# TensorE in the program's order in both mixers of a hybrid encoder layer, with other work dealt out between half steps

## The chip, the cores and the metric

The kernel runs on one NeuronCore of a Trainium2 chip. The metric is the device time of one launch in microseconds; lower is better.

## The reference, cut to what matters

One encoder layer over 1024 tokens of width 1024, in float32. The change touches the two attention mixers and the work that runs beside them.

```python
u = rms_norm(h); qa, ka, va, qb, kb, vb = split(u @ w_in)     # 1024 x 2304
# mixer A: 8 query heads, 2 key heads of 64, normed, rotary, over all keys
sc = einsum('bkgqd,bksd->bkgqs', qblk, k) * scale
oa = rms_norm(einsum('bkgqs,bksd->bkgqd', softmax(sc), v))
# mixer B: 8 heads, three dilated windows (128,1), (512,4), (2048,16), merged by their denominators
ob = rms_norm(einsum('pbhs,pbhsd->bhsd', softmax(lses), outs))
h = h + concat(oa, ob) @ w_out
h = h + hierarchical_moe(rms_norm(h))                          # 32 experts
y = rms_norm(h)
```

## The kernel before, in words

Every float32 matmul operand is split into a high and a low part (`split`: ScalarE copies the high part at L131, VectorE subtracts at L140), and a product is three (or two) matmuls. The program is written through Tile: the author traces instructions in program order, and the scheduler sets each engine's order from a simulated timeline, so that an instruction may pass earlier ones that are not ready in that simulation. `tc.manual_schedule(engines={PE})` around a region makes TensorE keep the program's order there; the routing and the experts behind the mixers (L1068 and L1250) already stand in such regions. The other engines' orders, and the DMA queues', are the scheduler's in either case.

The work before and in the mixers is written as Python generators, and a `yield` is a place where another generator may be let in.

- `job(n, jp)` (L254) projects one chunk of 256 columns of `w_in` for two tiles of tokens: 8 pieces of 6 matmuls of 256 columns each (L261 to L263), a `yield` after each, then the evacuation, the rotary on VectorE (L234, L237, L238) and the splits, and a last `yield`. Chunks 0 and 1 are run before the mixers, 4 jobs each; `rest_of_projection` runs the other 7, so 7 x 4 x 9 = 252 yields.
- Mixer A, `prepare_a` (from L489): turns a head's queries (L303, two pieces), finds each row's maximum over the keys (L499 matmul and L500 VectorE maximum, 8 pieces of two), then `shifts` makes the negative maximum (L333 to L335) and turns it in (two pieces). 12 yields a head.
- Mixer A, `steps_a`: a head has 16 steps (two blocks of 512 queries by 8 key tiles). `front` computes scores (L518, L519), ScalarE takes the exponential `p` and its high part `ph`, VectorE or GpSimd the low part `pl` (L445), GpSimd the running sum (L529). `back` multiplies the values (L536, L537). At kt = 7 it copies the block's output to `o` on ScalarE and turns it back right away, 4 times L543 and L544, then divides.
- Mixer B is alike: `prepare_b` (turning keys and queries, maxima L642 and L644; for head 0 the loads of `load_b`, L620 and L621, and then IDLE = 3 empty yields), `finish_b` (L662, L670, L673, then the shifts), and 8 steps a head: 4 strided ones (`front_c`, `back_c`), 4 windowed ones (`front_w`, `back_w`). The scores are masked on VectorE (L691), then `p` and `ph` on ScalarE, `pl` on GpSimd (L696). After the last window the sums are added (L762) and `divided` turns them (L740).
- `first_half` multiplies A's outputs by the first half of `w_out` (L827): 78 yields, 64 of them 3 matmuls of 512 columns.

`attend(n, stages, steps, ahead, pace)` (L448) weaves them: the stages of the first heads are run at once, then each step runs its `front`, the `back` of the step two before (ahead = 2), and `pace` pieces of the coming heads' preparation, and then yields once. `pace` is 1 in A and 3 in B. Around it stand three loops: A's turns with the projections (L555 on), RATE = 2.3 pieces a turn; A's remaining turns with one call into B's `attend` each (L770 on); B's turns with RATE_O = 1.0 piece of `first_half` each (L858 on), and then the rest of `first_half`.

[...]

Of the kernel before, what the change touches and what calls it, by code (L numbers as in the profile page):

```python
# [32 lines left out]
RATE = 2.3  # L33
# [7 lines left out]
RATE_O = 1.0  # L41
# [84 lines left out]
def tile_encoder(ctx, tc, I, out):  # L126
# [28 lines left out]
    turn = itertools.cycle(("i0", "i1"))  # L155
# [138 lines left out]
    def run(g):  # L294
        for _ in g:
            pass
# [70 lines left out]
    for j in range(NT):  # L367
        x, ss, _ = rows_x[j]
# [48 lines left out]
    def rest_of_projection():  # L417
        for n in range(2, 9):
            if n not in w_raw:
                load_chunk(n)  # L420
            split_chunk(n)
            if n + 1 < 9:
                load_chunk(n + 1)
            for jp in range(4):
                yield from job(n, jp)
# [3 lines left out]
    part = {"pl": SH_P, "s": 1.0}  # L429
# [18 lines left out]
    def attend(n, stages, steps, ahead, pace):  # L448


        state, at = {}, {}

        def stage(k, h):
            state[h] = yield from stages[k](h, state.get(h))

        def advance(g, times):
            for _ in range(times):
                if next(g, g) is g:
                    return False
            return True  # L460

        d = len(stages)
        for h in range(d):
            for k in range(d - h):
                yield from stage(k, h)
        waiting = []
        for h in range(n):
            coming = [stage(d - 1 - a, h + 1 + a) for a in range(d) if h + 1 + a < n]
            for front, back in steps(h, state.pop(h)):
                front()  # L470
                waiting.append(back)
                if len(waiting) > ahead:
                    waiting.pop(0)()
                for _ in range(pace):
                    if coming:
                        g = coming.pop(0)
                        if advance(g, 1):
                            coming.append(g)
                yield
            for g in coming:  # L480
                yield from g
        for back in waiting:
            back()
# [69 lines left out]


    turns = attend(8, [prepare_a], steps_a, 2, 1)  # L555
    side = rest_of_projection()
    due = 0.0
    while side is not None:
        next(turns, None)
        due += RATE  # L560
        while due >= 1:
            due -= 1
            if next(side, side) is side:
                side = None
                break
    part.update(pl=SH_P2, s=SH_S2)
    inx.close()
    obp = ctx.enter_context(tc.tile_pool(name="obp", bufs=1, side="right"))
# [116 lines left out]
    def steps_b(h, state):  # L685
# [61 lines left out]
        def back_w(j0):  # L747
# [20 lines left out]
            [(lambda j=j: front_w(j), lambda j=j: back_w(j)) for j in range(0, NT, 2)]  # L768

    side = attend(8, [prepare_b, finish_b], steps_b, 2, 3)  # L770
    for _ in turns:
        next(side, None)
    att.close()


# [55 lines left out]
    def first_half():  # L831
        for k in range(2):
            load_out(k)
        A.dma_start(g_o[0], _all(I["out_norm_a_g"], 512))
        A.dma_start(g_o[1], _all(I["out_norm_b_g"], 512))
        yield
        for k in range(4):
            split_out(k)
            if k < 3:
                load_out(2 + k)  # L840
            yield
        o = turned(q_a[:, 0], 0, "x")
        for j in range(NT):
            x = [wk_a.tile([P, 512], F32, name="x2") for _ in range(2)]
            for b in range(2):
                G.dma_start(x[b], _tokens(I["x"], j)[:, 512 * b:512 * b + 512])
            now = o
            if j + 1 < NT:
                o = turned(q_a[:, j + 1], 0, "x")
            yield  # L850
            for b, h in enumerate((q_a, h_b)):
                ps = bank("d", [P, 512])
                yield from half_product(0, now, ps, b)
                V.tensor_tensor(h[:, j], ps, x[b], op=OP.add)
        split_out(4)
        yield

    more, due = first_half(), 0.0  # L858
    for _ in side:
        due += RATE_O  # L860
        while due >= 1:
            due -= 1
            next(more, None)
    run(more)
    names.update(a="b", b="x", c="d", d="i1", s="i0")
    first_mixed = turned(o_b[0][:, 0], 1, "a")
    wka.close()
# [499 lines left out]
```

## Time and profile before

| what | us |
|---|---|
| median of 3 runs (1391.66 to 1401.73) | 1392.15 |
| the profiled execution | 1393.38 |
| its span, first to last instruction | 1391.7 |
| TensorE busy | 1303.2 |
| VectorE busy | 1152.4 |
| ScalarE busy | 926.2 |
| GpSimd busy | 568.6 |

A matmul's record runs from its start to its modelled end, and the next one starts before that end, so the time that a matmul takes from TensorE is the distance between starts. PE is TensorE's matmuls, PEld its weight loads, DVE VectorE, ACT ScalarE, POOL GpSimd, SP SyncE, whose queue issues most DMAs. L131 and L140 are helpers that many operations share, so their tiles tell them apart.

### The profile page before, as it was taken

The page shows a single profiled execution, that of the slowest core. Times are in us where ns is not written, and L with a number is a line of the kernel's source. Part 1 is how long each engine was busy: PE and PEld are TensorE (multiplying, and loading weights), DVE is VectorE, ACT ScalarE, POOL GpSimd, SP SyncE. Part 2 cuts the span into 40 slices and gives each one's busy share as a digit, 9 for nine tenths or more (in the row PEclk, how much of TensorE's full clock was granted, in tenths as well). Part 3 has the DMA queues.
Part 4 walks back from the last instruction along what each step waited for, and adds up shares of the span by engine and source line. Part 5 has one row for each costly group of instructions (what it writes and reads, how often), then busy time and mean ns, then how long its engine had stood idle before and what let it go on. Part 6 is the DMA issues. An engine that isn't in the chain of part 4 may idle for free. (4 is left out here: it accounts for less than half of the span.)

```text
span 1391.7 us, 21904 instructions
## 1 busy us (share of the span) xinstructions
PE 1303.2 (94%) x7333; PEld 1110.6 (80%) x7333; DVE 1152.4 (83%) x2001; ACT 926.2 (67%) x1366; POOL 568.6 (41%) x556
## 2 busy tenths in 40 slices
PE   5999899999998999999897999999999999999983
PEld 5999779888976889889686788878888888888862
DVE  5788997899868777667587799989999999999976
ACT  5334556655566656556443688878888888888873
POOL 5673566745566645446354611122111111111215
PEclk9999999999998999899998999999999999999997
DMA  7113321231242564445767999999999999999925
GB/s 258 62 39 85 84 68 54 61 75 36 58 138 60 145 186 117 112 128 164 278 210 240 308 371 367 353 341 372 360 351 351 345 360 355 349 353 342 376 74 226
DMA packets 213044, 299.63 MB, mean 215 GB/s; under 512 B 94307, under 2 KB 115939, under 8 KB 212928
## 3 DMA queue, kind: packets, MB, share of 16 engines
q1 hardware_dynamic: 200528, 272.91, 58.1%
q0 software_dynamic: 11968, 24.55, 6.7%
q8 instruction: 58, 0.95, 0.3%
q10 hardware_dynamic: 432, 0.75, 0.3%
q14 instruction: 58, 0.48, 0.1%
HBM read 267.85 MB, written 44.58 MB: 224 GB/s over the span
## 5 line engine op out<-in xcount | busy, mean ns | idle before, releaser
L140 DVE TENSOR_TENSOR wl<-unit,wh 128x1024 fp32r<-128x1024 f32 x140 | 168.4, 1223 | 21.1 <-ACT wh L131 20.1
L1163 POOL DMA_INDIRECT o_b<-xn_d,rows x32 | 51.4, 1606 | 303.1 <-PE ps_a L1180 300.8
L131 ACT ACTIVATE wh<-unit 128x1024 fp32r<-128x1024 f32 x140 | 147.3, 1062 | 36.3 <-PE ps_b L1196 12.5
L529 POOL TENSOR_TENSOR psum<-psum,p 128x512 f32<-128x512 f32 x93 | 138.0, 1484 | 66.7 <-ACT p L131 56.6
L263 PE MATMUL ps_i<-wih,ul 128*128 128x256 f32 x576 | 163.1, 283 | 1.2 <-DVE ul L140 1.2
L261 PE MATMUL ps_i<-wih,uh 128*128 128x256 f32 x576 | 162.7, 283 | 0.8 <-ACT uh L131 0.8
L262 PE MATMUL ps_i<-wil,uh 128*128 128x256 f32 x576 | 162.2, 282 | 0.0
L131 ACT ACTIVATE ph<-p 128x512 fp32r<-128x512 f32 x192 | 119.0, 630 | 12.7 <-DVE pl L445 5.7
L445 DVE TENSOR_TENSOR pl<-p,ph 128x512 fp32r<-128x512 f32 x93 | 96.1, 1035 | 24.7 <-ACT ph L131 24.6
L131 ACT ACTIVATE p<-ps_b 128x512 f32<-128x512 f32 x128 | 74.6, 595 | 62.2 <-PE ps_b L519 39.7
L261 PEld LDWEIGHTS ps_i<-wih,uh 128*128 128x128 f32 x576 | 109.6, 190 | 7.0 <-ACT uh L131 1.5
L262 PEld LDWEIGHTS ps_i<-wil,uh 128*128 128x128 f32 x576 | 109.4, 190 | 5.5
L263 PEld LDWEIGHTS ps_i<-wih,ul 128*128 128x128 f32 x576 | 109.5, 190 | 5.1 <-DVE ul L140 1.7
L696 POOL TENSOR_TENSOR pl<-p,ph 128x512 fp32r<-128x512 f32 x64 | 83.4, 1309 | 73.2 <-ACT ph L131 51.9
L1233 POOL DMA_INDIRECT y_d<-y,rows x31 | 50.3, 1622 | 137.5 <-ACT y L131 134.2
L140 DVE TENSOR_TENSOR wl<-rawc,wh 128x1024 fp32r<-128x1024 f32 x70 | 84.4, 1223 | 10.4 <-ACT wh L131 9.9
L500 DVE TENSOR_REDUCE m<-ps_x 128x1 f32<-128x512 f32 x128 | 84.9, 678 | 7.9 <-PE ps_x L499 7.6
L1196 PE MATMUL ps_b<-wh,x_hi 128*128 128x512 f32 x256 | 87.0, 421 | 0.0
L131 ACT ACTIVATE wh<-rawc 128x1024 fp32r<-128x1024 f32 x70 | 74.3, 1067 | 18.2 <-PE ps_b L1196 7.2
L1220 PE MATMUL ps_d<-wh,h_hi 128*128 128x512 f32 x256 | 81.0, 397 | 1.7 <-ACT h_hi L131 1.7
L1220 PE MATMUL ps_d<-wh,h_lo 128*128 128x512 f32 x256 | 81.1, 398 | 1.5 <-DVE h_lo L140 1.5
L1196 PE MATMUL ps_c<-wh,x_hi 128*128 128x512 f32 x256 | 80.9, 397 | 0.0
(326 smaller groups left out, 3888.9 us busy)
## 6 DMA issues: line engine op xcount, KB each, us to landing
unit<-in_w_up SPq DMA_DIRECT2D x49, 512.0 KB
unit<-in_w_gate SPq DMA_DIRECT2D x47, 512.0 KB
unit<-in_w_down SPq DMA_DIRECT2D x44, 512.0 KB
rawc<-in_w_gate SPq DMA_DIRECT2D x25, 512.0 KB
rawc<-in_w_down SPq DMA_DIRECT2D x23, 512.0 KB
rawc<-in_w_up SPq DMA_DIRECT2D x22, 512.0 KB
h_b<-in_w_down SPq DMA_DIRECT2D x19, 512.0 KB
raw<-in_w_in SPq DMA_DIRECT2D x36, 256.0 KB
```

What stands on the lines that cost most here:

```text
L131: A.activation(o, i, f, **kw)
L140: (eng or V).tensor_tensor(lo, src, hi, op=OP.subtract)
L261: T.matmul(ps[:, jj], u_hi[j][:, k], wh, start=(k == 0 and jj == 0), stop=False, skip_group_check=True)
L262: T.matmul(ps[:, jj], u_hi[j][:, k], wl, start=False, stop=False, skip_group_check=True)
L263: T.matmul(ps[:, jj], u_lo[j][:, k], wh, start=False, stop=(k == 7), skip_group_check=True)
L445: engine("pl").tensor_tensor(pl, p, ph, op=OP.subtract)
L500: V.tensor_reduce(m2[:, j, b:b + 1], ps, axis=AX.X, op=OP.max)
L529: engine("s").tensor_tensor(st["s"], st["s"], p, op=OP.add)
L696: G.tensor_tensor(pl, p, ph, op=OP.subtract)
L1163: gathers.append(G.indirect_dma_start(out=x_g, out_offset=None, in_=xn_d[:, :], in_offset=bass.IndirectOffsetOnAxis(ap=rows, axis=0), boun ...
L1196: T.matmul(st["gu"[n % 2]], lhs[:, k % 4], rhs[:, 512 * a:512 * a + 512], start=(k == 0 and i == 0), stop=(k == 7 and i == 2))
L1220: T.matmul(py[b], lhs[:, k], w[n][:, 512 * b:512 * b + 512], start=(k == 0 and i == 0), stop=(k == 3 and i == 2))
```

## The change

`attend` yields after each part of a step: with pace 1 the parts are front, piece, back; with pace 3 front, piece, back, piece, piece. The pieces thus stand between the halves, and what runs beside is let in after every part. The rates are divided by the number of parts, 3 in A's loop and 5 in B's, while the loop between the two calls B's `attend` once per part of A. IDLE stays 3. Around the three loops TensorE keeps the program's order.

```diff
--- before.py
+++ after.py
@@ -467,16 +467,20 @@
         for h in range(n):
             coming = [stage(d - 1 - a, h + 1 + a) for a in range(d) if h + 1 + a < n]
             for front, back in steps(h, state.pop(h)):
-                front()
                 waiting.append(back)
-                if len(waiting) > ahead:
-                    waiting.pop(0)()
-                for _ in range(pace):
+
+                def piece():
                     if coming:
                         g = coming.pop(0)
                         if advance(g, 1):
                             coming.append(g)
-                yield
+
+                turn = [front, lambda: waiting.pop(0)() if len(waiting) > ahead else None]
+                for i in range(pace):
+                    turn.insert(2 * i + 1, piece)
+                for part in turn:
+                    part()
+                    yield
             for g in coming:
                 yield from g
         for back in waiting:
@@ -555,14 +559,15 @@
     turns = attend(8, [prepare_a], steps_a, 2, 1)
     side = rest_of_projection()
     due = 0.0
-    while side is not None:
-        next(turns, None)
-        due += RATE
-        while due >= 1:
-            due -= 1
-            if next(side, side) is side:
-                side = None
-                break
+    with tc.manual_schedule(engines={mybir.EngineType.PE}):
+        while side is not None:
+            next(turns, None)
+            due += RATE / 3
+            while due >= 1:
+                due -= 1
+                if next(side, side) is side:
+                    side = None
+                    break
     part.update(pl=SH_P2, s=SH_S2)
     inx.close()
     obp = ctx.enter_context(tc.tile_pool(name="obp", bufs=1, side="right"))
@@ -768,8 +773,9 @@
             [(lambda j=j: front_w(j), lambda j=j: back_w(j)) for j in range(0, NT, 2)]
 
     side = attend(8, [prepare_b, finish_b], steps_b, 2, 3)
-    for _ in turns:
-        next(side, None)
+    with tc.manual_schedule(engines={mybir.EngineType.PE}):
+        for _ in turns:
+            next(side, None)
     att.close()
 
 
@@ -856,12 +862,13 @@
         yield
 
     more, due = first_half(), 0.0
-    for _ in side:
-        due += RATE_O
-        while due >= 1:
-            due -= 1
-            next(more, None)
-    run(more)
+    with tc.manual_schedule(engines={mybir.EngineType.PE}):
+        for _ in side:
+            due += RATE_O / 5
+            while due >= 1:
+                due -= 1
+                next(more, None)
+        run(more)
     names.update(a="b", b="x", c="d", d="i1", s="i0")
     first_mixed = turned(o_b[0][:, 0], 1, "a")
     wka.close()
```

## Rows read from the trace of the kernel before

**Rows 1.** The page, parts 1 and 2: busy time, and the clock of TensorE in 40 equal slices.

```profile
PE 1303.2 (94%) x7333; PEld 1110.6 (80%) x7333; DVE 1152.4 (83%) x2001; ACT 926.2 (67%) x1366; POOL 568.6 (41%) x556
...
PEclk9999999999998999899998999999999999999997
```

**Rows 2.** Stretch, length; busy us of PE, PEld, DVE, ACT, POOL; clock; DMA; GB/s.

```profile
95.60:165.70 70.10, 64.81 (x453) 58.83 (x453) 65.79 (x130) 31.55 (x57) 32.22 (x30) 0.98 0.37 83
165.70:393.40 227.70, 220.92 (x1501) 197.10 (x1500) 193.95 (x305) 140.15 (x249) 139.54 (x96) 1.00 0.24 58
393.40:451.80 58.40, 52.08 (x269) 39.88 (x268) 47.98 (x90) 40.15 (x73) 41.52 (x32) 0.91 0.39 109
451.80:660.80 209.00, 200.97 (x1255) 183.64 (x1255) 148.99 (x434) 127.29 (x219) 104.86 (x101) 0.93 0.53 141
660.80:680.90 20.10, 15.03 (x72) 11.70 (x70) 11.84 (x29) 8.56 (x14) 8.44 (x17) 0.83 0.75 244
```

**Rows 3.** Waits of PE, 130 to 681 us: total us, times, longest.

```profile
PE ps_x L499 <- DVE m L500: 5.1, 8, 1.8
PE ps_d L537 <- DVE pl L445: 4.4, 7, 1.2
...
PE ps_x L543 <- DVE m L500: 2.9, 1, 2.9
PE ps_b L705 <- DVE p L691: 2.9, 2, 1.6
...
PE ps_b L518 <- ACT p L131: 1.6, 2, 1.1
...
PE ps_b L731 <- DVE p L691: 0.3, 1, 0.3
```

**Rows 4.** Timeline from 396.8 us: start, us, engine, line, what.

```profile
396.86 0.40 PE L537 MATMUL ps_d<-pl,v_st 128*64 128x512 f32 x1
...
397.09 0.28 PE L261 MATMUL ps_i<-wih,uh 128*128 128x256 f32 x1
...
397.20 0.28 PE L262 MATMUL ps_i<-wil,uh 128*128 128x256 f32 x1
...
397.36 0.59 ACT L131 ACTIVATE o<-ps_d 128x512 f32<-128x512 f32 x1
...
398.72 0.33 PE L543 MATMUL ps_x<-eye,o 128*128 128x64 f32 x2
```

**Rows 5.** L263 by stretch (two are one piece), and the row maxima of head 0.

```profile
0.00:86.00 86.00, 44.98 (x154) 30.32 (x155) 0.96 0.42 142
86.00:104.00 18.00, 11.39 (x41) 7.58 (x41) 1.00 0.06 16
...
L500 DVE TENSOR_REDUCE m<-ps_x x18: 674/678/692, 91.2 to 125.0; 128x1 f32<-128x512 f32 x18
```

**Rows 6.** DMA issues, L518 and the DMA share when mixer B begins.

```profile
398.01 0.33 SPq L620 DMA_DIRECT2D keep<-bk_d  x1
...
393.40:422.90 29.50, 6.54 (x16) 3.03 (x16) 0.94 0.71 197
...
399.00:403.00 4.00, 4.00 (x29) 3.49 (x29) 2.79 (x6) 3.41 (x7) 3.44 (x3) 1.00 0.80 254
403.00:408.00 5.00, 4.89 (x21) 3.23 (x20) 5.00 (x9) 3.72 (x8) 3.59 (x3) 1.00 1.01 318
408.00:411.00 3.00, 2.68 (x11) 1.68 (x11) 3.00 (x5) 1.80 (x3) 1.68 (x4) 1.00 0.04 11
```

**Rows 7.** Groups by line and form between scores and weights in mixer B, 451 to 661 us.

```profile
L696 POOL TENSOR_TENSOR pl<-p,ph 128x512 fp32r<-128x512 f32 x62 | 80.8, 1309 | 71.9 <-ACT ph L131 50.5 <-issue 6.0 <-PE ps_i L720 3.6
L691 DVE TENSOR_TENSOR p<-ps_b,masks 128x512 f32<-128x512 f32 x63 | 43.2, 686 | 13.7 <-PE ps_b L706 7.4 <-POOL pl L696 3.7 <-PE ps_b L732 2.6
L131 ACT ACTIVATE ph<-p 128x512 fp32r<-128x512 f32 x67 | 41.6, 628 | 2.7 <-PE ps_i L720 1.6
...
L762 DVE TENSOR_TENSOR ob<-ob,ps_i 65x320 f32<-65x320 f32 x7 | 3.3, 475 | 0.2 <-PE ps_i L760 0.2
```

## The prediction, made before the changed kernel was built or run

> **What bounds the kernel now.** I read the page first, then the busy time by stretch, then the list of waits, and last the timeline at the places where the new order differs. The page [rows 1] says that TensorE is busy 94% of the span and that its granted clock stays near 9 tenths or full except in a few slices. The change touches only the mixers, so I cut them into five stretches [rows 2]: the start of mixer A (95.6 to 165.7 us), its steady part with projections beside it (165.7 to 393.4), the stretch in which A ends and mixer B is prepared (393.4 to 451.8), mixer B (451.8 to 660.8), and the end of the output product's first half (660.8 to 680.9). In the steady part TensorE is busy 220.92 of 227.70 us at full clock, VectorE 193.95. So TensorE is the bound there and waits only 3%. At the start VectorE is the fuller one (65.79 of 70.10). In B TensorE is busy 200.97 of 209.00 us, but at a mean clock of 0.93.
>
> What could be won is small. All waits that are put down to an instruction between 130 and 681 us sum to 30.5 us over 18 rows, the first and the last of which are shown, and five of them make 16.9 [rows 3]. [...]
>
> **The change part by part.** The work is the same, instruction for instruction; what moves is TensorE's order. Now the scheduler mixes: after the last value product of a block (L537 at 396.86) other matmuls go before the turning matmuls L543 at 398.72 that need its copy `o` [rows 4]. The change makes TensorE follow the program inside three regions, and the program has places where the next matmul needs what another engine makes from the one just before.
>
> *Turning the output of mixer A (`back`, kt = 7).* L543 stands right behind L537, with no yield between. In the shown case `o` ends 1.09 us after L537 starts (396.86 to 397.95) [rows 4]; L537 fills 0.23 of it (the spacing from it to L261), so TensorE stands 0.86 us, and about 0.05 for the signal. That is the floor. ScalarE is busy 61% of the steady part [rows 2], and a copy that finds `p` and `ph` ahead of it waits up to 1.2 us more. 16 blocks at 0.9 give 14 us, at 2.1 give 34; I take 1.1, near the floor since the shown case is an ordinary one: 18 us. Of it 2.9 us is paid already (L543) [rows 3], so **+15**.
>
> *The start of A.* In the order of before TensorE runs ahead with projections while VectorE prepares head 0. Two L263 make one piece (a `yield` of `job`), so 77 pieces are done by 86.0 us and 20.5 more from 86 to 104 [rows 5], where the program before the loop holds 2 chunks of 32 = 64. So 13 pieces were pulled ahead, and 34 are spent before 104. In the new order the preparation of head 0 has 12 yields, and each brings RATE/3 = 0.77 piece: 9 pieces. The 25 others are 150 matmuls of 0.115 us (the spacing of L261 and L262) [rows 4], 17 us without cover. Against that: the stretch is VectorE's. Its 16 row maxima cost 16 x 0.678 = 10.8 us [rows 5], and with fewer projections ahead fewer rotaries stand in its queue, so the first steps come earlier and the pieces serve as cover later. Both ends stand, 0 and 17; I take **+6**, nearer to 0 because VectorE, busy 65.79 of 70.10 us, is the fuller engine there.
>
> *The preparation of mixer B.* The loads of head 0 are issued from 398.0, right behind the last projection, and the DMA engines are full until 408 [rows 6]. They are hidden by IDLE = 3 empty yields. Before, a yield is one step of A, 1.84 us apart there (16 L518 in 29.5 us), so some 5.5 us, and what waits can be passed. After the change a yield is a third of a step, so the three cover 1.9 us, and the turning of the keys then stands at TensorE's head, with A's steps queued behind it. The keys are a quarter of the 2 MB, so they land some 2 us after the transfers begin at 399, the queries later. Between 0 and 408 - 398 - 3 = 7 us; I take **+4**.
>
> *The end of each head of B (`divided`).* The second group of transposes needs VectorE's add L762 of the last window, right behind L760: about 0.28 - 0.12 (a matmul of 256 columns and its spacing, as L261) + 0.48 (L762) + 0.1, less 0.24 for the first group's transposes, is 0.5 us [rows 4, 7]. Eight heads: **+4**, 0 to 10 with none of it or another VectorE operation ahead.
>
> *B's steps without pieces.* The 15 pieces of preparation fall, at 3 a step, into a head's first 5 steps. In the last 3 the way from scores to `pl` is 0.3 (matmul) + 0.69 (mask) + 0.63 (`p`, as long as `ph`) + 0.63 (`ph`) + 1.31 (`pl`) = 3.6 us and four signals [rows 7], and it is covered by two steps of some 1.9 us each, which the new order cannot lengthen. 24 steps at 0 to 0.7; I take 0.15: **+4**.
>
> *The row maxima's last piece*, after which the transposes of `shifts` and `finish_b` wait for four short VectorE operations, stands 16 times in the same order as before; those that were passed by other work now wait. 0 to 10, I take **+3**.
>
> *What goes away.* Fronts, pieces and backs now stand a third of a step apart with projections between them, so the waits for the maxima (L499, 5.1 us), for `pl` (L537, 4.4), for the masks' sums (L705, 2.9) and for `p` (L518, 1.6) should shrink [rows 3]; and TensorE standing elsewhere gives VectorE time. From 0 to -15; I take **-12**. The clock I leave at 0: even feeding would give back up to 23 us, new waits would cost up to 15.
>
> *The rates.* RATE/3 and RATE_O/5 keep the pieces per step. When the projection ends about 22 steps of A are left where it was 30 (252 pieces, less 9, at 2.3 a step), and three yields a step bring 67 calls into B, 26 of them its preparation and 41 for 8 steps; before, 30 calls, 4 steps. So 4 pieces more are left to the end, where one more half product stands: its matmuls are the same work, and its add (0.7 us) has the next tile's transposes beside it: 0, at most +2. DMA issues (the loads of `load_b`, `load_v`, of `x2`) stay in SP's and GpSimd's own orders, which the regions do not pin; they pass no other transfer by the change, and beyond the load above they are covered by a whole head.
>
> Sum: 15 + 6 + 4 + 4 + 4 + 3 - 12 = +24 us. The profiled execution took 1393.4 us around its span of 1391.7, 1.2 above the median of the runs shown (1392.15). So 1393.4 + 24 = 1417.4, which I give as 1417.
>
> The list of waits shows TensorE standing for L537 and L499 with work behind them that was ready [rows 3]. [...]
>
> **The rivals.** *Faster, 0.17.* Even feeding holds the clock in B. For it: half-speed stretches there are 14% of 209 us [rows 2], in stretches with little beside the steps, and the change deals the output product out at five places a step where it was one. Against it: the same light matmuls remain. With the clock's 23 us back, the waits 12 less, and only the turning (15) paid beside the start at 0, the sum is -20: 1373. It decides at a granted clock of 0.97 or more in B.
>
> *No change, 0.27.* In A VectorE is busy 85 to 94% [rows 2]: what TensorE loses at the turning and at the start it would have lost later waiting for maxima and `pl`. Then 15 + 6 fall away: 1393 + 3 = 1396. Against it: in the steady part TensorE waits only 7 us of 228, too little to hold 15.
>
> *Slower than forecast, 0.13.* The short waits in B pull the clock down. For it: B already falls to half speed while TensorE is busy 96% of the time [rows 2]. With 0.85 instead of 0.93 the 209 us become 229, and with 0.5 us at the 24 late steps +8 more: 1417 + 20 + 8 = 1445. [...]
>
> **How the numbers follow.** Forecast 0.43, faster 0.17, no change 0.27, slower still 0.13. A measurement of this kernel tells about 1% (14 us) from no change. Faster by over 1% is nearly all of the first rival and a little of the forecast's lower end: 0.17. Within 1%: most of the second and the forecast's lower part: 0.28. Slower: 0.55. The likeliest case alone runs from 1400 (turning at its floor, B's terms at 0) to 1440 (turning at 1.6 us, start at 12, load at 7). The range reaches from 1380, which leaves out most of the faster case, to 1458, the upper end of the slower one with its waits doubled.
>
> **What would show it.** Right: an L543 wait for `o` near 1 us in 16 places; about 9 pieces between the first maxima and the first front, and TensorE idle there; a wait of L303 for the key load at B's start; a shorter list for L499 and L537. Wrong: a granted clock of 0.97 in B, or a steady part of A no longer per step than now while L543 waits, which would mean that VectorE set its pace.

## The result, and the profile after

The changed kernel takes 1498.74 us (median of four runs, 1492.74 to 1504.82) where the kernel before, on the same chip, takes 1393.30: a ratio of 1.0744, 95% interval 1.067 to 1.0818. It is slower, as forecast, but by 105 us and not by 24. The profile is of a run of 1504.82 us, so it shows some 6 us more than the median.

In the changed kernel the lines below the diff stand 4 to 7 lower: L499, L518, L537 and L543 are now L503, L522, L541 and L547, and in mixer B L642, L662, L740 are L647, L667, L745. The page, parts 1 and 2, beside [rows 1]:

```profile
PE 1352.3 (90%) x7333; PEld 1146.5 (76%) x7333; DVE 1139.3 (76%) x1999; ACT 932.9 (62%) x1366; POOL 557.0 (37%) x558
...
PEclk9989898998999586999999979999999999999997
```

TensorE runs the same 7333 matmuls and is busy 49 us longer with them. Nothing was added, so they ran slower: in the first half, where the mixers are, the digits of the clock now show a 5, a 6 and five 8s, where they showed two 8s.

To see where, I cut both kernels at the same events, from 78 us, up to where the two run alike: the first scores of A, the last projection, the last value product of A, the last scores of B, and the last matmul of the output product's first half (L827, now L833). Columns as in [rows 2]. First the kernel before:

```profile
78.00:95.70 17.70, 17.70 (x149) 17.44 (x148) 15.50 (x40) 4.21 (x6) 13.37 (x19) 1.00 0.15 44
95.70:397.70 302.00, 289.93 (x1979) 259.63 (x1979) 260.60 (x434) 174.15 (x310) 173.52 (x127) 0.99 0.26 63
397.70:465.30 67.60, 61.28 (x314) 48.48 (x313) 56.22 (x111) 47.45 (x86) 50.98 (x38) 0.90 0.41 117
465.30:660.70 195.40, 187.37 (x1182) 171.16 (x1181) 139.79 (x413) 117.44 (x201) 93.45 (x92) 0.93 0.54 143
660.70:668.40 7.70, 7.70 (x44) 6.47 (x44) 3.58 (x5) 4.95 (x8) 3.08 (x3) 1.00 0.69 236
sum 590.40, PE 563.98 PEld 503.17 DVE 475.69 ACT 348.19 POOL 334.40; mean PE 112.80 PEld 100.63 DVE 95.14 ACT 69.64 POOL 66.88
```

And the changed one:

```profile
78.00:102.70 24.70, 14.20 (x81) 12.02 (x81) 17.84 (x38) 4.47 (x8) 5.67 (x8) 0.79 0.13 36
102.70:472.50 369.80, 337.61 (x2122) 297.27 (x2121) 267.49 (x459) 190.49 (x328) 185.64 (x146) 0.92 0.22 51
472.50:561.40 88.90, 71.40 (x346) 57.88 (x344) 49.81 (x136) 48.11 (x89) 41.30 (x35) 0.75 0.40 113
561.40:759.10 197.70, 170.29 (x1049) 157.26 (x1048) 120.05 (x360) 108.07 (x183) 85.61 (x85) 0.89 0.49 127
759.10:785.60 26.50, 21.27 (x98) 15.58 (x96) 10.97 (x27) 6.45 (x12) 10.22 (x21) 0.94 0.74 258
sum 707.60, PE 614.77 PEld 540.01 DVE 466.16 ACT 357.57 POOL 328.44; mean PE 122.95 PEld 108.00 DVE 93.23 ACT 71.52 POOL 65.69
```

The five stretches grew by 7.0, 67.8, 21.3, 2.3 and 18.8 us, 117.2 in all (the rest of the kernel is 5.7 shorter). B and what follows it belong together: B holds 133 matmuls fewer, 54 more are left behind it. The sum rows split the growth in two. TensorE is busy 614.77 us where it was 563.98, **51 us more** for almost the same matmuls (3696 and 3668): that is the clock. It stands still for 92.8 us (707.60 - 614.77) where it was 26.4, **66 us more**: those are waits. The clock column says the first part again. In both traces the clock stands at 1.00 or at 0.50: in the changed kernel it is 1.00 from 196 to 201 us, 0.50 from 201.5 to 204.5 and 1.00 from 205 to 210, in the kernel before 0.50 from 577 to 585 and 1.00 from 586 to 600. So 2 x (1 - clock) x length is the time at half speed: 59 us in the stretch of the projections, where it was 6, and 160 over all five, where it was 47; half of the difference, an estimate of 57 us, is lost.

The waits of PE from 78 to 800 us, total, times, longest; before they summed to 30.5 us [rows 3], now to 93.9. Of the accumulators in the mixers `ps_x` takes maxima and turnings, `ps_b` scores, `ps_d` the values of A, `ps_i` projections and later the values of B.

```profile
PE ps_x L547 <- ACT o L131: 23.8, 16, 4.5
PE ps_x L303 <- DVE keep L685: 12.3, 5, 5.1
PE ps_x L303 <- ACT q_st L131: 9.1, 1, 9.1
PE ps_x L503 <- DVE m L504: 6.8, 9, 2.1
PE ps_x L303 <- DVE q1b L685: 6.8, 3, 3.7
PE ps_x L303 <- DVE ql_st L335: 5.8, 4, 3.5
...
PE ps_x L667 <- DVE mx L663: 4.8, 2, 3.2
PE ps_i L745 <- DVE ob L767: 3.8, 8, 0.9
PE ps_x L647 <- DVE mc L649: 3.5, 1, 3.5
PE ps_i L765 <- POOL pl L701: 3.0, 6, 0.9
...
PE ps_d L541 <- POOL pl L445: 2.0, 2, 1.2
...
PE ps_b L522 <- ACT p L131: 0.6, 1, 0.6
```

The turning of A's output waits in all 16 blocks, 1.5 us each in the mean (0.7 to 4.5). What one such wait does shows in the timeline of the changed kernel: start, us, engine, line, and in brackets the idle time before.

```profile
196.29 0.40 PE L541 MATMUL ps_d<-pl,v_st 128*64 128x512 f32 x1
198.34 0.43 PE L547 MATMUL ps_x<-eye,o 128*128 128x64 f32 x2 [1.65 <-ACT o L131]
...
200.82 0.28 PE L262 MATMUL ps_i<-wil,uh 128*128 128x256 f32 x1
200.94 0.28 PE L263 MATMUL ps_i<-wih,ul 128*128 128x256 f32 x1
...
202.44 0.41 PE L263 MATMUL ps_i<-wih,ul 128*128 128x256 f32 x1
202.66 0.41 PE L261 MATMUL ps_i<-wih,uh 128*128 128x256 f32 x1
```

TensorE stands for 1.65 us. At 200.8 the projections still start 0.12 us apart, the distance of [rows 4]; at 202.4 they start 0.22 apart, and at 204.8 the old distance is back. So the clock fell some 3 us after the wait, with TensorE at work again. Three other waits for `o`, behind the value products at 221.6, 333.3 and 444.4 us, with 12 us around each; the clock is the seventh number of a row after its stretch, 0.72, 0.74 and 0.72. Not every wait has such a fall behind it: around the one of 0.76 us at 310.2 us the clock is 1.00 (last row).

```profile
220.00:232.00 12.00, 9.40 (x47) 8.38 (x46) 3.83 (x9) 4.78 (x8) 3.77 (x3) 0.72 0.22 45
332.00:344.00 12.00, 9.29 (x49) 8.11 (x48) 6.22 (x11) 6.11 (x11) 3.80 (x3) 0.74 0.33 68
443.00:455.00 12.00, 10.68 (x55) 9.37 (x55) 4.97 (x7) 4.80 (x9) 2.56 (x2) 0.72 0.14 45
...
308.00:320.00 12.00, 11.24 (x84) 10.05 (x84) 7.36 (x14) 7.48 (x14) 4.76 (x4) 1.00 0.28 79
```

### The profile page after: what moved, and what is told of

The parts are those of the page before. It is cut to its first block, busy times and chain, and to the rows that moved or that the text cites. A ratio compares the mean times of both kernels' runs of the same rounds, so it can differ in the third digit from the quotient of the medians.

```text
span 1503.2 us, 21877 instructions
## 1 busy us (share of the span) xinstructions
PE 1352.3 (90%) x7333; PEld 1146.5 (76%) x7333; DVE 1139.3 (76%) x1999; ACT 932.9 (62%) x1366; POOL 557.0 (37%) x558
## 5 line engine op out<-in xcount | busy, mean ns | idle before, releaser
L533 POOL TENSOR_TENSOR psum<-psum,p 128x512 f32<-128x512 f32 x94 | 127.9, 1361 | 166.6 <-ACT p L131 141.1
L261 PE MATMUL ps_i<-wih,uh 128*128 128x256 f32 x576 | 170.4, 296 | 0.8 <-ACT uh L131 0.8
L263 PE MATMUL ps_i<-wih,ul 128*128 128x256 f32 x576 | 168.7, 293 | 1.3 <-DVE ul L140 1.3
L262 PE MATMUL ps_i<-wil,uh 128*128 128x256 f32 x576 | 167.6, 291 | 0.0
L261 PEld LDWEIGHTS ps_i<-wih,uh 128*128 128x128 f32 x576 | 116.2, 202 | 13.6 <-ACT uh L131 1.5
L445 DVE TENSOR_TENSOR pl<-p,ph 128x512 fp32r<-128x512 f32 x92 | 92.8, 1010 | 41.3 <-ACT ph L131 41.2
L262 PEld LDWEIGHTS ps_i<-wil,uh 128*128 128x128 f32 x576 | 115.7, 201 | 9.0
L263 PEld LDWEIGHTS ps_i<-wih,ul 128*128 128x128 f32 x576 | 115.6, 201 | 1.8 <-DVE ul L140 1.8
L131 ACT ACTIVATE wh<-rawc 128x1024 fp32r<-128x1024 f32 x70 | 74.3, 1067 | 18.2 <-PE ps_b L1203 7.6
L1203 PE MATMUL ps_b<-wl,x_hi 128*128 128x512 f32 x256 | 81.8, 401 | 0.0
```

Of the source, the lines that this page charges most:

```text
L131: A.activation(o, i, f, **kw)
L261: T.matmul(ps[:, jj], u_hi[j][:, k], wh, start=(k == 0 and jj == 0), stop=False, skip_group_check=True)
L262: T.matmul(ps[:, jj], u_hi[j][:, k], wl, start=False, stop=False, skip_group_check=True)
L263: T.matmul(ps[:, jj], u_lo[j][:, k], wh, start=False, stop=(k == 7), skip_group_check=True)
L445: engine("pl").tensor_tensor(pl, p, ph, op=OP.subtract)
L533: engine("s").tensor_tensor(st["s"], st["s"], p, op=OP.add)
```

## The experiments

The theories. **Clock** (C in the expectations): the new waits are paid twice, by their own length and again by half speed behind them. Its rival, **waits** (W): TensorE's standing is the whole loss, and the lower clock only shows it. Then **queue** (Q): what TensorE waits for is not the operation but its place in another engine's queue, so that a wait taken away at one place comes back at the next; its rival is that each wait has a price of its own that goes away with it. Theory D says that VectorE sets the pace of mixer A whatever TensorE does. All ratios are to the kernel before on the same chip, with 95% intervals.

### One wait removed, and one wait filled

The first kernel runs the turning of A's output one step later, at the start of the next `back`, so that `o` has a whole step to be copied in.

```diff
                     act(o, po)
-                    ps = bank("x", [P, 4, P])
+                    def turned_back():
+                        ps = bank("x", [P, 4, P])
...
+                    later.append(turned_back)
...
             def back(kt, b=b, st=st):
+                if later:
+                    later.pop(0)()
```

> The changed kernel, with the turning of mixer A's block (L547 and L551 of the changed kernel) run one step later, at the head of the next step's back, so that ScalarE's copy o has a whole step. Theory C (each wait of a microsecond or more in the fixed order is paid twice, once as the wait and again as a stretch at half clock behind it): the 23.8 us of waits for o go and with them the nine half-speed stretches that start within 4 us of them in mixer A (some 50 us at half speed, 25 us lost): about 45 us off, 1498 to 1453. Theory W (the waits alone cost, the low clock falls where TensorE would stand anyway): 20 to 24 us off, about 1476. Theory D (VectorE sets the pace of mixer A): within 8 us of the changed kernel.

Measured: 1501.88 us, 1.0762 (1.072 to 1.0804); nothing gained. The waits for `o` did go, from 23.8 us to 4.1. But the transposes of `shifts` now wait 35.2 us for `ql_st`, eight times, up to 7.1, where it was 5.8 us. So the run decides nothing between C and W, and its time is the one that D expected.

The second kernel leaves the order as the change has it and adds work: 6 matmuls of 512 columns ahead of each turning, into the bank that the turning then overwrites. They run while `o` is copied.

```diff
                     ps = bank("x", [P, 4, P])
+                    for i in range(FILL):
+                        T.matmul(ps.rearrange("p i c -> p (i c)"), k2[:, 0:128], q2[:, qs], ...)
```

> The changed kernel, with 6 matmuls of 512 columns whose result is overwritten put before the turning's matmuls at each of the 16 places, so that TensorE works about 1.4 us there instead of standing; nothing else moves. Work is added, so theory W expects 0 to 5 us slower than the changed kernel (1498 to 1503), and so does theory D. Theory C expects the half-speed stretches behind the 16 waits to shrink from about 50 us to under 20, and the time to fall by 10 to 20 us in spite of the added work (about 1483).

Measured: 1479.02 us, 1.0617 (1.0569 to 1.0665): 20 us faster than the change, with 96 matmuls more. The stretch of the projections, beside 369.80 us at 0.92 above:

```profile
103.30:450.90 347.60, 331.19 (x2195) 292.28 (x2193) 272.83 (x459) 190.13 (x328) 189.59 (x146) 0.99 0.23 55
```

It is 22 us shorter at a clock of 0.99. The fill hardly brings `o` sooner: five waits for it are left, 4.5 us together, where the 16 waits of the changed kernel, each less the 1.4 us of its fill (6 x 0.23), would leave 7.0 in five; by this estimate `o` comes 2.5 us sooner in all. What it does is keep TensorE at work. So the half speed is a cost of its own, which W and D do not have: shown for region 1.

### Which part of the change

Three kernels carry the dealing out (the new `attend` and rates) with fewer fixed regions, and one the fixed regions without the dealing. The edit is the same at each region:

```diff
-    with tc.manual_schedule(engines={mybir.EngineType.PE}):
+    if True:
```

Only the first region (A with the projections) fixed:

> The changed kernel with the program's order kept in the first region alone (mixer A beside the projections); the other two regions are the scheduler's again, and the dealing stays. By the stretches of the two traces the first region costs 60 to 75 us of the 105 and the others 40 to 50. Theory C and W: about 1450. If the dealing were the cause (theory R), the time would stay near 1498.

Measured: 1460.47 us, 1.0473 (1.0434 to 1.0512).

No region fixed, the dealing alone:

> The changed kernel's dealing without any region of fixed order. Theory C and W (the fixed order is the cause): within 20 us of the kernel before, 1375 to 1415. Theory R (the dealing and the rates are the cause: head 0 of A starts without projections beside it, IDLE covers a third of a step each): 1440 or more.

Measured: 1410.37 us, 1.0107 (1.0063 to 1.0151).

The second and third regions fixed, with the dealing:

> The changed kernel with the scheduler's order in the first region and the program's in the other two (the end of mixer A with mixer B's preparation, and mixer B). If the parts add (dealing 17, first region 50 more by the run with it alone, the rest 38): 1410 + 38 = about 1448. If the waits of the first region are paid once for all and B's own are hidden without them: under 1425.

Measured: 1451.02 us, 1.0412 (1.038 to 1.0444).

All three fixed, with `attend` and the rates of before:

> The kernel before with the program's order on TensorE in the same three regions, and no dealing: one yield a step, the rates and the pieces as before. Theory C and Q (a fixed order leaves TensorE standing behind another engine's queue, and projections between the parts are cover): without the dealing the cover is lumped behind the back, so the time is that of the changed kernel or worse, 1490 to 1540. Theory R (the dealing and its rates cost, as the run without regions showed with 17 us): 1470 to 1485.

Measured: 1475.74 us, 1.0603 (1.0562 to 1.0645).

The parts add up. The dealing costs 17 us (1410.4 - 1393.3); on top of it the first region's order costs 50 (1460.5) and that of the other two 41 (1451.0); 1410.4 + 50 + 41 = 1501, where the whole takes 1498.7. The fixed order is most of the loss, and it is not for want of dealing: without it, it costs 82 us.

### Whose queue it is

In the first kernel, with the turning moved, the wait for `ql_st` is the largest. Its timeline, VectorE's operations between the last maxima and the transpose:

```profile
194.36 1.27 DVE L504 TENSOR_REDUCE m<-ps_x 128x1 f32<-128x512 f32 x2
...
195.56 0.67 DVE L140 TENSOR_TENSOR stage<-stage,sth 128x512 fp32r<-128x512 f32 x1
...
196.16 1.75 DVE L445 TENSOR_TENSOR pl<-p,ph 128x512 fp32r<-128x512 f32 x1
...
197.83 1.75 DVE L140 TENSOR_TENSOR wil<-raw,wih 128x512 fp32r<-128x512 f32 x1
199.50 0.15 DVE L507 TENSOR_TENSOR m<-m 128x8 f32<-128x8 f32 x1
199.58 0.68 DVE L140 TENSOR_TENSOR wil<-raw,wih 128x512 fp32r<-128x512 f32 x1
...
200.18 0.16 DVE L333 TENSOR_SCALAR negm<-m 128x8 f32<-128x8 f32 x1
200.38 0.17 DVE L334 CAST ql_st<-negm 128x8 fp32r<-128x8 f32 x1
200.59 0.17 DVE L335 TENSOR_TENSOR ql_st<-negm,ql_st 128x8 fp32r<-128x8 f32 x1
...
200.81 0.64 PE L303 MATMUL ps_x<-eyer,ql_st 128*66 128x128 f32 x4 [5.78 <-DVE ql_st L335]
```

The four short operations that make `ql_st` take 0.65 us. They come some 4 us late because three splits and a `pl`, 0.67 to 1.75 us each, stand ahead of and between them in VectorE's queue. TensorE, held at the transpose for 5.78 us, meanwhile issues none of the work behind it.

If that is so, empty pieces between the maxima and the transposes should let A's steps through until VectorE gets there:

```diff
         V.tensor_tensor(ql[:, :, 65], t, ql[:, :, 64], op=OP.subtract)
+        for _ in range(empty):
+            yield
...
-        q1 = yield from shifts(ql, m, qst)
+        q1 = yield from shifts(ql, m, qst, 3 if h else 0)
```

> The kernel with the turning one step later, and besides 3 empty pieces between a head's last row maximum and the transposes of its shifts (from head 1 on), so that VectorE's four short operations have three more steps, some 8 us. In the run before, taking away the wait for o (24 us) put 35 us of waits for ql_st in its place: TensorE reaches the shifts sooner, and four other VectorE operations stand ahead of them in VectorE's order. Theory Q (in a fixed order the wait is for another engine's queue and goes to the next tight place unless that has distance too): the 35 us fall under 8, with the half-speed stretches behind them, 40 to 60 us off, about 1450. Theory D (VectorE sets the pace of mixer A, and TensorE's waits add up to the same whatever place they take): 1490 or more, with the waits at the maxima (L504) grown to 20 us or more.

Measured: 1452.67 us, 1.0411 (1.0379 to 1.0443), 49 us below the kernel that it was built on and far below the 1490 of D, which falls with it. The wait for `ql_st` falls from 35.2 to 3.1 us, and nothing of its size takes its place. The stretch of the projections falls from 377.30 to 332.80 us, more than the wait, and again with the clock (0.90 to 0.98); first the moved turning, then this one:

```profile
102.00:479.30 377.30, 336.54 (x2122) 299.96 (x2120) 270.56 (x459) 190.72 (x328) 185.18 (x146) 0.90 0.21 50
```

```profile
102.40:435.20 332.80, 315.84 (x2122) 281.63 (x2120) 273.67 (x459) 188.59 (x328) 190.65 (x146) 0.98 0.24 57
```

The other way to bring the two queues together is to put VectorE in the program's order as well in that region, on the kernel with the moved turning:

```diff
-    with tc.manual_schedule(engines={mybir.EngineType.PE}):
+    with tc.manual_schedule(engines={mybir.EngineType.PE, mybir.EngineType.DVE}):
```

> The kernel with the turning one step later, where in the first region VectorE keeps the program's order too, so the shifts' four operations follow the last row maximum without other operations between them, but every low part also waits in its own place for ScalarE. Theory Q: the waits for ql_st fall from 35 to under 15 us and the time by 15 to 40 us (1460 to 1485) unless VectorE's own waits eat it. Theory D: no gain, 1495 or more, as VectorE only loses freedom.

Measured: 1566.85 us, 1.1239 (1.1204 to 1.1274): a miss, it costs 65 us more. That is what D expected, but it is VectorE's new waits that cost it. VectorE now waits where it used to pass. Its largest wait from 78 to 800 us was 51.0 us, 23 times, in the kernel without this edit, and is here

```profile
DVE pl L445 <- ACT ph L131: 108.8, 49, 6.6
```

and TensorE, in turn, stands 39.5 us for the maxima (6.5 before this edit) and still 29.2 for `ql_st`:

```profile
PE ps_x L503 <- DVE m L504: 39.5, 18, 5.6
PE ps_x L303 <- DVE ql_st L335: 29.2, 7, 7.2
```

### Distance everywhere

The next kernel gives every wait of the list above some distance: the two edits before, 12 projection pieces ahead of head 0 and the full rate beside it, IDLE 12, two and three empty pieces in `finish_b`, `divided` one step later, RATE_O 1.35.

```diff
-IDLE = 3
+IDLE = 12
-RATE_O = 1.0
+RATE_O = 1.35
...
+        for _ in range(12):
+            next(side)
...
+                later_b.append(lambda: [divided(b) for b in range(2)])
```

> The changed kernel with distance at each place where its trace shows TensorE standing: the turning of A one step later and 3 empty pieces ahead of the shifts (as in the run at 1452 us); 12 pieces of projection ahead of head 0's preparation and the full RATE beside it; IDLE 12; in finish_b 2 empty pieces ahead of the first small product and 3 ahead of its last transposes; the division of B one step later; RATE_O 1.35, so that no half products are left to the end. Theory Q: what the program's order costs is these places alone, so the start gives 8, the preparation of B 16, B 17 and the end 18 us: 1393 plus or minus 15. Theory S (a fixed order costs in itself, since no static place fits the other engines' queues): the waits move on again and the time stays above 1420.

Measured: 1435.57 us, 1.0303 (1.0256 to 1.035). This is a miss for Q and the outcome that theory S named. Distance heals A, where the clock is 1.00 up to the last projection, and not what follows. The two stretches behind it, up to the last scores of B, take 309.5 us for 1532 matmuls, where 263.0 us held 1496 before. In B TensorE's largest wait is now 6.5 us in four places at a value product (L745), for which the profile names no releaser, and the clock is 0.91 (0.89 in the changed kernel, 0.93 before).

Two smaller questions went with it. Is it IDLE that makes the dealing cost 17 us (three thirds of a step are less cover than three steps)? The dealing alone, with IDLE 9:

> The dealing without regions of fixed order (1410 us), with IDLE 9 in place of 3, so that the empty yields cover three steps of A as before the change. If the 17 us of the dealing lie in the preparation of B that begins two steps too early: 1393 to 1400. If they lie in the start of A or in the dealing itself: 1405 or more.

Measured: 1409.01 us, 1.0111 (1.0064 to 1.0157), the same as with 3. IDLE is not it.

And does the dealing help the fixed order? The fixed order with `attend` of before, the turning moved and the 3 empty pieces:

> The kernel before with the program's order in the three regions and no dealing (1476 us), with the turning one step later and 3 empty pieces ahead of the shifts. Theory Q: the same two places cost here too, 1430 to 1450. If the dealing's projections between the halves are worth their name as cover: it stays 15 us or more behind the run with dealing and the same gaps (1452), at 1467 or more.

Measured: 1441.6 us, 1.0342 (1.0285 to 1.04), 11 us less than the same with the dealing (1452.7), though the two intervals overlap a little. It does not.

Last, the best of the parts together: fixed order, dealing and distance in the first region alone; B as before.

```diff
-    def attend(n, stages, steps, ahead, pace):
+    def attend(n, stages, steps, ahead, pace, dealt=True):
...
-steps_b, 2, 3)
+steps_b, 2, 3, False)
```

> The program's order and the dealing in the first region alone, with the distances given there (12 pieces of projection ahead, the full RATE beside head 0's preparation, the turning one step later, 3 empty pieces ahead of the shifts); behind it mixer B undealt and in the scheduler's order, as in the kernel before. Theory Q for the first region and the rest of the loss in B's fixed order: the projections end near 396 us with 92 steps done where the kernel before has 98 at 398, 6 steps of 1.84 us behind, so 1393 + 9 = about 1402, within 1393 to 1412. Theory S (a fixed order costs in itself also here): above 1420. Faster than before by 1% or more would mean that the clock, full through the first region, gives back more than the scheduler's freedom.

Measured: 1402.95 us, 1.0058 (1.0035 to 1.0082). From its first full step on, to the end of B:

```profile
117.30:396.30 279.00, 271.22 (x1859) 240.93 (x1858) 239.47 (x392) 164.60 (x287) 152.07 (x110) 1.00 0.28 65
396.30:489.70 93.40, 85.49 (x445) 67.70 (x443) 69.60 (x152) 63.20 (x116) 62.00 (x46) 0.89 0.35 99
489.70:666.90 177.20, 170.35 (x1074) 157.30 (x1073) 130.77 (x376) 107.81 (x186) 87.74 (x86) 0.92 0.57 149
```

With distance TensorE runs at full clock in the fixed order too: the clock is 1.00 and the projections end at 396.3 us, where they ended at 397.7. But 92 steps of A are done by then, not 98 (the scores' matmuls counted). They are lost at the start: from 117.3 to 396.3 us TensorE runs 1859 matmuls, where it ran 1799 before. In the kernel with distance everywhere, which has this first region too, the waits for `ql_st` (one of 4.9 us) and `q_st` (one of 1.7) are left; before, none stood from 78 to 117.3 us. These six steps, some 11 us at 1.84 each, are left for the stretch behind, where 93.4 us stand against 67.6 before (B's own stretch is 18.2 us shorter); in the end 7 us are missing. None of the twelve kernels of the experiments beats the one before.

## Why the prediction was right in sign and wrong in size

**The step that failed is "the clock I leave at 0".** I had set up to 23 us of gain against up to 15 of loss, and cancelled them. No run shows either. The 23, which the 1373 of the faster rival uses too, is an estimate: half of the 47 us at half speed that 2 x (1 - clock) x length gives for the last three stretches of [rows 2]; for the 15 I gave no working. What the change showed in their place is 51 us more in the sum of matmul time. By the clock column nearly half of the loss (53 of the 113 us more at half speed) lies in the stretch with projections, whose steady part ran at 1.00 before [rows 2] and to which I gave no clock term. The slower rival had the mechanism, but in B alone: its 0.85 there was 0.89, and most of the loss was elsewhere. In the stretch of the projections the clock is 0.92 with waits for `o` of 1.5 us in the mean, and 0.99 with the same waits filled.

**The waits came to 66 us and not to 24.** The sum's +24 was all waits. By the terms of the sum:

- The turning of A's output: 18 us forecast, 23.8 measured, in 16 of 16 blocks. Right in kind, and near in size; the 0.05 for the signal is what the trace has (0.05 or 0.06 us from the end of `o` to L547 in each block); the copy stood behind others on ScalarE (in the wait behind 333.3 us, behind a copy of `q` and the 1.05 us of `q_st`).
- The start of A: +6 forecast, too small. The stretch is 7.0 us longer (24.70 and 17.70 us) but holds 68 matmuls fewer, which are left for later. It has one wait of 9.1 us for `q_st`, and 2 x 0.21 x 24.7 = 10.4 us at half speed, half of them lost: some 14 us, near the 17 of my upper end. The wait stands ahead of the first maxima; between these and the first front, where I had looked for it, TensorE waits under 2 us.
- The last piece of the maxima, ahead of `shifts` and `finish_b`: **+3 forecast, some 21 measured** (`ql_st`, `keep` and `q1b` at L303, 24.9 us, where the same waits were 4.2). I counted four short operations and forgot the queue that they stand in, though I had counted one for `o`. This is the largest miss among the waits; the moved turning shows how large it can get (35.2). The first small product of `finish_b` waits besides for `mx`, 4.8 us where it was 1.0, which the sum did not have.
- What goes away: **-12 forecast, about -5 measured**. Waits for `p` fell to 0.6 from 4.5 (two rows), those of L541 for `pl` to 2.0 from 4.4, but those of L503 for the maxima rose from 5.1 to 6.8 [rows 3].
- `divided`: +4 forecast, 3.8 measured (`ob`, eight times). B's late steps: 4 forecast, 3.0 at L765, where it was 1.4.
- The preparation of B: 4 forecast and 3.5 measured, but not for the load that I named, so the size is luck. TensorE waited for a masked maximum (`mc`). On VectorE a `pl` of 1.75 us stood ahead of it, and then it waited 1.05 us for the masks, whose issue at 483.14 us stood behind those of `keep`, at 472.83 to 481.12, on SP's queue (changed kernel, timeline):

```profile
483.14 0.35 SPq L632 DMA_DIRECT2D masks<-in_masks  x1
...
487.86 0.42 DVE L649 CUSTOM_DVE_ANT_0 junk<-ps_x,masks 128x256 f32<-128x256 f32 x1 [1.05 <-DMA masks<-in_masks]
```

- The rates: 0 to +2 forecast, but the tail after B grew by 18.8 us. 22 steps of A were left at the projections' end, as forecast. But B's stretch is 2.3 us longer with 133 matmuls fewer in it, and the tail holds 54 more; 37 of these are half products, where I had forecast 4 pieces, which are 12.

**The rivals.** "VectorE sets the pace of A anyway" falls: with the waits for `o` filled the stretch is 22 us shorter, so TensorE does set it. "Even feeding holds the clock in B" falls too: 0.93 became 0.89, and with the dealing alone it is 0.93 again (third row below). For one reading of mine [rows 3] are not enough: they give the waits, not what stood ready behind them. The timeline of the kernel before gives that for one wait of each line. L537 starts at 191.94 us after 1.18 us for `pl`; L536, the next matmul, needs a `ph` that was done by 190.59. L499 starts at 201.82 after 0.55 us for the maxima; L262, the next, needs a `wil` that was done by 201.17.

**What stays open.** What in the dealing itself costs 17 us: not IDLE. With the dealing alone the three large stretches run

```profile
90.30:422.10 331.80, 313.69 (x2082) 279.93 (x2081) 286.99 (x466) 183.18 (x327) 192.28 (x140) 0.97 0.24 57
422.10:499.80 77.70, 67.55 (x360) 57.86 (x359) 53.62 (x138) 47.05 (x87) 45.96 (x36) 0.82 0.48 129
499.80:680.10 180.30, 174.24 (x1085) 158.96 (x1084) 129.13 (x367) 106.89 (x184) 86.27 (x87) 0.93 0.53 145
```

so the loss lies ahead of B and goes with a lower clock (0.97 and 0.82, where it was 0.99 and 0.90); its cause was not found. Nor was it settled why the fixed order behind the first region, which costs 41 us, resists distance; a kernel with B's VectorE work reordered by hand was not tried.

## What to carry to other kernels

In this kernel pinning one engine to the program's order made its waits places in some other engine's queue: cost a wait by what stands ahead in that queue, not by the few operations that are waited for, and expect it to turn up at the next tight place when it is removed. On TensorE allow for the clock beside the waits (here 51 us beside 66), above all in a stretch that runs at full clock, and test that cheaply by filling a wait with matmuls whose result is thrown away. Before pinning, give each hand-over (copy then transpose, maximum then transpose) a step of distance in the program; only with that did a kernel with a pinned region come within 0.6% of the one before, and none passed it.

## What the hardware showed that was not expected

The clock of TensorE fell in stretches that were mostly busy: in the changed kernel it was 0.50 from 201.5 to 204.5 us, with TensorE busy all 3.00 us, and 0.72 from 443 to 455, with 10.68 of 12.00 busy. In one place standing for 1.65 us was followed, some 3 us later and with TensorE at work, by matmuls of 256 columns 0.22 us apart where they had been 0.12; over 12 us around three other waits the mean granted clock is 0.72 to 0.74, around another 1.00. Work added in these waits, 96 matmuls, made the kernel 20 us faster (1479.02 and 1498.74).
